# A fused two-block kernel on one core: the 3x3 convolution's taps as one chain on VectorE, without GpSimd's partial sums

## The chip, the cores and the metric

The kernel runs on one core of a Trainium2 chip, in one launch. The metric is the device time in microseconds (us). The engines are named as the profile names them: PE is TensorE's matmuls and PEld its weight loads, DVE is VectorE, ACT is ScalarE, POOL is GpSimd, SP is SyncE, which issues most DMAs. Each engine takes its instructions strictly in the order in which they stand in its queue.

## What is computed

Two transformer-like blocks over 512 tokens of width 1024. The first has two linear-attention branches, GLA (gated linear attention) and GDN (a gated delta rule), after a context of 256 tokens; the second is a sparse-attention layer, run twice, and is not touched here. The place of the change is the GDN branch's input:

```python
def conv_grid(u, w):                       # u: 512 tokens as an 8 x 64 grid, 1536 channels
    ug = u.reshape(b, rows, GRID_W, ch)
    out = lax.conv_general_dilated(ug, w[:, :, None, :], window_strides=(1, 1), padding='SAME', ...,
                                   feature_group_count=ch)
    return out.reshape(b, t, ch)

qkv = jnp.concatenate([bq, bk, bv], axis=-1)
qkv = jax.nn.silu(conv_grid(qkv, gdn_conv) if on_grid else conv_seq(qkv, gdn_conv))
bq = l2norm(qkv[..., :GDN_QK]...) * (GDN_DK ** -0.5)
bk = l2norm(qkv[..., GDN_QK:2 * GDN_QK]...)
bv = qkv[..., 2 * GDN_QK:]
```

Each channel is convolved with its own 3 x 3 taps, in float32. The context's tokens get a one-dimensional convolution of three taps (`conv_seq`). Behind it the delta rule needs, per chunk of 64 tokens, the products of k and q, the inverse of a triangular matrix, and a chain over the chunks.

## The kernel before, in words

Channels lie on the 128 partitions, so the 1536 convolved channels are 12 blocks, one per head and kind (4 of k, 4 of v, 4 of q). `conv_block` (L871) handles one: it loads and splits a weight tile (each float32 weight is split into a high and a low part, `split`, L188: ACT copies the high part, L190, and POOL or DVE subtracts, L193), projects the context and the 512 tokens on PE, and convolves. `convs` (L931) calls it for the heads of one half (`pp`), in the order k, v, q, and turns the results with PE transposes into the layouts that the delta rule wants. Two calls of `convs` alternate with two of `gla` in `first_block`: gla 0, convs 0, gla 1, convs 1; then `gla_out`, `gdn_scores`, `gdn_inverses`, `gdn_chains`, and the projections of gates (`fillers`, L485), which need only weights and the normed input.

The two-dimensional convolution of one block works on a zero-padded tile `xpad` of 10 x 66 per channel. ACT copies the projection into it (L897) and makes the centre tap from PSUM (L904). The other eight taps are on three engines: POOL makes the first tap (L908), the third (L914) and two additions (L915) into a partial sum `th`, ACT makes the second tap into `tap` (L912), DVE adds five taps one after the other (L918) and at the end the partial sum (L919). Then `silu2` (L395) runs a tanh on ACT (L398, into the same buffer `th`, which exists once) and a product on DVE (L399).

The GLA's levels (L837 to L861) put their differences and products on DVE (L837, L838, L840), exponentials on ACT and the keys' part on POOL (L847 to L850). `gdn_scores` (L984) loads rows of decays by DMA (L998, a buffer that exists once), subtracts and bounds them on DVE (L1030, L1032, L1037) and copies the scores KQ (L1020). `gla_out` scales the GLA's output on DVE (L623, transposed by PE right after) and multiplies it with its gate (L630). `gdn_inverses` is a chain of 62 small DVE operations that ends with two transposes (L1077).

The order of the instructions on each engine isn't that of the code: a scheduler places them when the program is built, with an estimate of its own of how long each takes (the `TileContext` of L1704). So a changed instruction moves others, on other engines too, as the section on the change shows.

Of the kernel before, what the change touches and what calls it, by code (L numbers as in the profile page):

```python
# [10 lines left out]
F32 = mybir.dt.float32  # L11
F32R = mybir.dt.float32r
I32 = mybir.dt.int32
AF = mybir.ActivationFunctionType
ALU = mybir.AluOpType
# [3 lines left out]
P = 128  # L19
D = 1024  # L20
KT = D // P
T = 512
# [210 lines left out]
def project(k, w, h, n=T, c0=0, tag="mm", step=None):  # L233

    ps = k.ps(tag)
    h = [x if isinstance(x, list) else [x[:, kt] for kt in range(x.shape[1])] for x in h]
    m = len(h[0])
    step = step or k.step
    for a in range(0, n, step):
        b = min(a + step, n)  # L240
        for kt in range(m):
            three(k, ps[:, a:b], w(kt, c0, P), [x[kt][:, a:b] for x in h], kt == 0, kt == m - 1)
    return ps[:, :n]
# [151 lines left out]
def silu2(k, out, x, tmp=None):  # L395

    tmp = out if tmp is None else tmp
    k.nc.scalar.activation(tmp, x, AF.Tanh, scale=0.5)  # L398
    k.nc.vector.scalar_tensor_tensor(out, tmp, 1.0, x, op0=ALU.add, op1=ALU.mult)  # L399
# [471 lines left out]
def conv_block(k, pool, win, hx, hc, blk, y, out, bank):  # L871


    nc = k.nc
    V, A, G = nc.vector, nc.scalar, nc.gpsimd
    w = Weights(k, win, [(1568 + P * blk, P, 0)])
    if hc is not None:
        th = k.t(pool, [P, T], F32, tag="th", bufs=1)
        pad = k.t(pool, [P, TC + 2], F32, tag="cpad", bufs=1)
        G.memset(pad[:, 0:1], 0.0)  # L880
        G.memset(pad[:, TC + 1:TC + 2], 0.0)
        A.copy(pad[:, 1:TC + 1], project(k, w, hc, TC, tag=bank))
        acc = y[:, :X0]
        for j in (1, 0, 2):
            s = k.conv[:, 3 + j, blk:blk + 1]
            if j == 1:
                V.tensor_scalar(acc, pad[:, j:j + TC], s, None, op0=ALU.mult)
            else:
                V.scalar_tensor_tensor(acc, pad[:, j:j + TC], s, acc, op0=ALU.mult, op1=ALU.add)
        silu2(k, acc, acc, th[:, :X0])  # L890
    pad = k.t(pool, [P, 10, 66], F32, tag="xpad", bufs=2)
    G.memset(pad[:, 0:1], 0.0)
    G.memset(pad[:, 9:10], 0.0)
    G.memset(pad[:, 1:9, 0:1], 0.0)
    G.memset(pad[:, 1:9, 65:66], 0.0)
    ps = project(k, w, hx, T, tag=bank).rearrange("p (r c) -> p r c", c=64)
    A.copy(pad[:, 1:9, 1:65], ps)  # L897

    def tap(j):
        return pad[:, j // 3:j // 3 + 8, j % 3:j % 3 + 64], k.conv[:, j, blk:blk + 1]  # L900

    acc = y[:, -T:].rearrange("p (r c) -> p r c", c=64)
    part = k.t(pool, [P, T], F32, tag="th", bufs=1).rearrange("p (r c) -> p r c", c=64)
    A.activation(acc, ps, AF.Copy, scale=tap(4)[1])  # L904
    for n, j in enumerate((0, 1, 2)):
        src, c = tap(j)
        if n == 0:
            G.tensor_scalar(part, src, c, 0.0, op0=ALU.mult, op1=ALU.add)  # L908
        else:
            one = k.t(pool, [P, T], F32, tag="tap", bufs=1).rearrange("p (r c) -> p r c", c=64)  # L910
            if n == 1:
                A.activation(one, src, AF.Copy, scale=c)  # L912
            else:
                G.tensor_scalar(one, src, c, 0.0, op0=ALU.mult, op1=ALU.add)  # L914
            G.tensor_tensor(part, part, one, op=ALU.add)  # L915
    for j in (3, 5, 6, 7, 8):
        src, c = tap(j)
        V.scalar_tensor_tensor(acc, src, c, acc, op0=ALU.mult, op1=ALU.add)  # L918
    V.tensor_tensor(acc, acc, part, op=ALU.add)  # L919
    a, b = y[:, -T:], k.t(pool, [P, T], F32, tag="th", bufs=1)  # L920
    if out is not None:
        a, b = (z.rearrange("p (t i) -> p t i", i=P) for z in (a, b))
    silu2(k, a if out is None else out, a, b)
# [7 lines left out]
def convs(k, pool, win, hx, hc, pp, s):  # L931
# [6 lines left out]
    for hd in (2 * pp, 2 * pp + 1):  # L938
        y = k.t(pool, [P, TA], F32, tag="y", bufs=2)
        conv_block(k, pool, win, hx, hc, 4 + hd, y, None, f"cm{pp}")  # L940
        rk = k.t(pool, [P, 6], F32, tag="rk", bufs=2)
        for a, n in ((0, 2), (2, 4)):
            ps = k.ps("tr")
            for t in range(n):
                tr(k, ps[:, t * P:(t + 1) * P], y[:, (a + t) * P:(a + t + 1) * P])
            for t in range(n):
                junk = k.t(pool, [P, NT, P], F32, tag="sq", bufs=1)[:, 0]
                A.activation(junk, ps[:, t * P:(t + 1) * P], AF.Square, accum_out=rk[:, a + t:a + t + 1])
            power(k, rk[:, a:a + n], rk[:, a:a + n], 1.0, 4 * EPS)
            V.tensor_tensor(kn[:, a:a + n, hd], ps[:, :n * P].rearrange("p (t d) -> p t d", d=P),  # L950
                            bc(rk[:, a:a + n, None], [P, n, P]), op=ALU.mult)
            ps = k.ps("tr")
            for t in range(n):
                tr(k, ps[:, t * P:(t + 1) * P], kn[:, a + t, hd])
            if a:
                A.copy(by_tile(kq[:, hd])[:, :, 0:4:3],
                       ps.rearrange("p (t u j) -> p t u j", u=2, j=64))
            else:
                A.copy(kc[:, hd], ps[:, :n * P])
    for hd in (2 * pp, 2 * pp + 1):  # L960
        y = k.t(pool, [P, TA], F32, tag="y", bufs=2)
        conv_block(k, pool, win, hx, hc, 8 + hd, y, None, f"cm{pp}")
        for a, n in ((0, 2), (2, 4)):
            ps = k.ps("tr")
            for t in range(n):
                tr(k, ps[:, t * P:(t + 1) * P], y[:, (a + t) * P:(a + t + 1) * P])
            A.activation(v[:, a:a + n, hd], ps[:, :n * P].rearrange("p (t d) -> p t d", d=P), AF.Copy, scale=0.5)
    for hd in (2 * pp, 2 * pp + 1):
        y = k.t(pool, [P, TA], F32, tag="y", bufs=2)
        q = by_tile(kq[:, hd])[:, :, 1:3].rearrange("p t u j -> p t (u j)")  # L970
        conv_block(k, pool, win, hx, None, hd, y[:, :T], q, f"cm{pp}")
        ps = k.ps("tr")
        sq = k.t(pool, [P, NT, P], F32, tag="sq", bufs=1)
        A.activation(sq, q, AF.Square)
        for t in range(NT):
            mm(k, ps[:, t:t + 1], sq[:, t], k.ones[:, 0:1])
        r = k.t(pool, [P, NT], F32, tag="rqh", bufs=2)
        power(k, r, ps[:, :NT], 1.0, 4 * EPS)
        for u in range(2):
            G.tensor_scalar(rq[64 - 64 * u:128 - 64 * u, :, hd], r[64 * u:64 * u + 64], 128.0 ** -0.5, 0.0,  # L980
                            op0=ALU.mult, op1=ALU.add)
# [726 lines left out]
```

## Time and profile before

| | |
|---|---|
| runs | 1330.84, 1329.47, 1330.38 us; median 1330.38 |
| profiled execution | 1328.28 us, span 1326.5 us, mean granted clock of TensorE 0.98 |
| PE busy | 1252.3 us, 94% |
| DVE busy | 867.2 us, 65% |
| ACT busy | 623.1 us, 47% |
| POOL busy | 431.8 us, 33% |

The span goes from the first to the last instruction of one profiled execution; that execution's own time is 1.8 us longer. A busy share is an average over stages with different limits; the stages are read with the view of windows. A group's row gives the mean of one instruction; the shortest one of a line shows what it takes undisturbed. Waits are put down to the instruction that came last.

### The profile page before, as it was taken

How to read it: one execution, taken by the hardware profiler on the slowest of the kernel's cores; microseconds unless marked ns; L12 is line 12 of the kernel's file. 1: busy time of each engine (PE TensorE's matmuls, PEld its weight loads, DVE VectorE, ACT ScalarE, POOL GpSimd, SP SyncE). 2: the span in 40 equal slices, each digit the busy share in tenths (PEclk: the TensorE clock that was granted, in tenths of full speed). 3: DMA queues.
4: the chain of work that ended last, by engine and by line, in shares of the span. 5: the costliest groups of instructions: out<-in, count | busy, mean ns of one | idle time of the engine just before them, and what ended most of it. 6: DMA issues, size and time to landing. Idle time of an engine off the chain costs nothing.

```text
span 1326.5 us, 22525 instructions
## 1 busy us (share of the span) xinstructions
PE 1252.3 (94%) x8290; PEld 1010.0 (76%) x8290; DVE 867.2 (65%) x1938; ACT 623.1 (47%) x1544; POOL 431.8 (33%) x469
## 2 busy tenths in 40 slices
PE   5998998989799999999899899999999999999997
PEld 1587987889799888587688778667777887667776
DVE  2748998698979974455767437654766537555664
ACT  2465445444452221244444336745655437645652
POOL 2416756376742322133423311111123311011131
PEclk9999999998999999999899999999999999999999
DMA  9421111202334321333553841012114631012121
GB/s 327 161 87 49 49 33 32 64 18 62 95 97 115 89 79 51 119 89 118 178 205 80 227 100 50 1 33 56 57 52 106 155 73 48 1 40 51 54 72 72
DMA packets 156766, 114.13 MB, mean 86 GB/s; under 512 B 37265, under 2 KB 137144, under 8 KB 156656
## 3 DMA queue, kind: packets, MB, share of 16 engines
q1 hardware_dynamic: 152888, 105.96, 27.8%
q10 hardware_dynamic: 3480, 6.65, 1.5%
q8 instruction: 65, 1.06, 0.3%
q14 instruction: 45, 0.37, 0.1%
q0 software_dynamic: 288, 0.09, 0.0%
HBM read 105.28 MB, written 10.27 MB: 87 GB/s over the span
## 4 chain that ended last, share of the span: by engine, by line
PE 71%; DVE 15%; DMA 4%; ACT 4%; issue 3%; POOL 2%; SPq 1%; POOLq 0%; ACTq 0%; DVEq 0%
PE A L172 30%; PE B L172 15%; PE C L172 9%; PE D L172 7%; PE E L172 6%; PE C L176 3%; DVE y L918 2%; DMA t<-w_mod 1%; DVE wlo L193 1%; DMA X<-cmp_w 1%; DVE aqe L823 1%; DVE att L861 1%; DVE a L838 1%; DVE a L837 1%; DVE a L840 1%
## 5 line engine op out<-in xcount | busy, mean ns | idle before, releaser
L172 PE MATMUL A<-t,whi 128*128 128x256 f32 (+1 forms) x1344 | 300.2, 314 | 3.7 <-DVE fill L399 2.2
L193 POOL TENSOR_TENSOR wlo<-wraw,whi 128x512 fp32r<-128x512 f32 x94 | 128.8, 1371 | 377.4 <-ACT whi L190 271.4
L190 ACT CAST whi<-wraw 128x512 fp32r<-128x512 f32 x226 | 139.1, 620 | 218.6 <-PE A L172 71.4
L172 PEld LDWEIGHTS A<-t,whi 128*128 128x128 f32 x1344 | 219.7, 191 | 24.4 <-issue 10.0
L172 PE MATMUL A<-t,wlo 128*128 128x256 f32 (+1 forms) x672 | 211.6, 315 | 0.7 <-POOL wlo L193 0.6
L193 DVE TENSOR_TENSOR wlo<-wraw,whi 128x512 fp32r<-128x512 f32 x132 | 107.3, 816 | 77.2 <-ACT whi L190 73.6
L172 PEld LDWEIGHTS A<-t,wlo 128*128 128x128 f32 x672 | 128.2, 191 | 14.2 <-issue 6.3
L172 PE MATMUL A<-whi,t 128*128 128x256 f32 (+1 forms) x544 | 122.0, 312 | 7.3 <-ACT av L765 4.4
L172 PE MATMUL C<-t,whi 128*128 128x256 f32 (+1 forms) x560 | 123.3, 311 | 0.0
L1436 ACT ACTIVATE X<-X,mx 128x256 f32<-128x256 f32 (+3 forms) x160 | 84.4, 528 | 41.2 <-DVE mx L1430 39.9
L172 PEld LDWEIGHTS A<-whi,t 128*128 128x128 f32 x544 | 90.9, 195 | 14.5 <-ACT av L765 4.8
L172 PEld LDWEIGHTS C<-t,whi 128*128 128x128 f32 x560 | 92.4, 193 | 6.6 <-issue 1.8
L172 PE MATMUL C<-t,wlo 128*128 128x256 f32 (+1 forms) x280 | 86.5, 310 | 0.0
L172 PE MATMUL A<-wlo,t 128*128 128x256 f32 (+1 forms) x272 | 83.7, 310 | 1.8 <-DVE wlo L193 1.6
L918 DVE SCALAR_TENSOR_TENSOR y<-xpad,t,y 128x512 f32<-128x512 f32 x60 | 65.2, 1087 | 4.6 <-ACT y L904 3.7
L176 PE MATMUL C<-t,X 128*128 128x128 f32 x352 | 57.8, 280 | 1.0 <-ACT pt L1447 0.4
L172 PEld LDWEIGHTS A<-wlo,t 128*128 128x128 f32 x272 | 53.1, 196 | 5.3 <-DVE wlo L193 2.2
L172 PEld LDWEIGHTS C<-t,wlo 128*128 128x128 f32 x280 | 54.1, 193 | 3.7 <-issue 1.4
L176 PEld LDWEIGHTS C<-t,X 128*128 128x128 f32 x352 | 40.2, 141 | 15.6 <-issue 6.5
L172 PE MATMUL B<-t,whi 128*128 128x512 f32 x144 | 47.6, 411 | 1.0 <-ACT whi L190 1.0
L1447 ACT COPY pt<-C 128x128 f32<-128x128 f32 (+3 forms) x96 | 39.0, 422 | 20.3 <-PE C L176 19.6
L1430 DVE CUSTOM_DVE_ANT_0 X<-B,t,sink 128x256 f32<-128x256 f32 (+1 forms) x64 | 27.1, 448 | 29.1 <-PE B L172 22.6
(621 smaller groups left out, 2811.4 us busy)
## 6 DMA issues: line engine op xcount, KB each, us to landing
wraw<-w_in SPq DMA_DIRECT2D x156, 256.0 KB
t<-w_mod SPq DMA_DIRECT2D x16, 512.0 KB
wraw<-w_out SPq DMA_DIRECT2D x32, 256.0 KB
t<-fill SPq DMA_DIRECT2D x20, 256.0 KB
wraw<-w_mod SPq DMA_DIRECT2D x16, 256.0 KB
wraw<-w_gdn_out SPq DMA_DIRECT2D x16, 256.0 KB
wraw<-w_o SPq DMA_DIRECT2D x16, 256.0 KB
X<-cmp_w SPq DMA_DIRECT2D x16, 256.0 KB
```

What stands on the lines that cost most here:

```text
L172: return k.nc.tensor.matmul(out, lhsT, rhs, start=start, stop=stop, **kw)
L176: return k.nc.tensor.transpose(out, in_, k.ident[:in_.shape[0], :in_.shape[0]])
L190: k.nc.scalar.copy(hi, raw)
L193: eng.tensor_tensor(lo, raw, hi.bitcast(F32), op=ALU.subtract)
L823: V.tensor_tensor(qe[64 * d:64 * d + 64, h], qT[hs], e[hs], op=ALU.mult)
L837: V.tensor_tensor(q4[:, :, 1], b4[:, :, 1], bmid, op=ALU.subtract)
L838: V.tensor_tensor(q4[:, :, 0], cmid, c4[:, :, 0], op=ALU.subtract)
L840: V.tensor_tensor(eq, eq, qT, op=ALU.mult)
L918: V.scalar_tensor_tensor(acc, src, c, acc, op0=ALU.mult, op1=ALU.add)
L1430: k.nc.vector.tensor_tensor_reduce(X[:, :n], ps[:, :n], mask, scale=-scale, scalar=first, op0=ALU.add, op1=ALU.min, accum_out=acc)
L1436: k.nc.scalar.activation(X, X, AF.Exp, bias=acc, scale=-1.0, accum_out=total)
L1447: k.nc.scalar.copy(pt[:, :n * P], ps[:, :n * P])
```

## The change

In `conv_block` all eight taps besides the centre become one chain of `scalar_tensor_tensor` on DVE. POOL's partial sum, ACT's second tap, their two buffers and DVE's last addition are gone. Per block that is three DVE operations more and one fewer, four POOL operations and one ACT operation fewer; there are 12 blocks. What is computed is the same sum in another order. Behind line 903 the changed kernel's line numbers are lower: L918 is L906 there, and from L919 on 13 less (L1030 is L1017, L1032 L1019, L1037 L1024, L1020 L1007).

```diff
     acc = y[:, -T:].rearrange("p (r c) -> p r c", c=64)
-    part = k.t(pool, [P, T], F32, tag="th", bufs=1).rearrange("p (r c) -> p r c", c=64)
     A.activation(acc, ps, AF.Copy, scale=tap(4)[1])
-    for n, j in enumerate((0, 1, 2)):
-        src, c = tap(j)
-        if n == 0:
-            G.tensor_scalar(part, src, c, 0.0, op0=ALU.mult, op1=ALU.add)
-        else:
-            one = k.t(pool, [P, T], F32, tag="tap", bufs=1).rearrange("p (r c) -> p r c", c=64)
-            if n == 1:
-                A.activation(one, src, AF.Copy, scale=c)
-            else:
-                G.tensor_scalar(one, src, c, 0.0, op0=ALU.mult, op1=ALU.add)
-            G.tensor_tensor(part, part, one, op=ALU.add)
-    for j in (3, 5, 6, 7, 8):
+    for j in (0, 1, 2, 3, 5, 6, 7, 8):
         src, c = tap(j)
         V.scalar_tensor_tensor(acc, src, c, acc, op0=ALU.mult, op1=ALU.add)
-    V.tensor_tensor(acc, acc, part, op=ALU.add)
```

The scheduler's order moves with it. First DVE, where the two q convolutions of the first half meet the start of the second GLA half (`ac` and `a` are the GLA's cumulated decays, L638 their first step). Before:

```order
L918 SCALAR_TENSOR_TENSOR y_1767<-xpad_1780,t_138,y_1767 128x512 x5
L919 TENSOR_TENSOR y_1767<-y_1767,th_1835 128x512
L399 SCALAR_TENSOR_TENSOR t_94<-th_1850,y_1767 128x4x128
L918 SCALAR_TENSOR_TENSOR y_1865<-xpad_1878,t_138,y_1865 128x512 x5
L256 TENSOR_SCALAR rqh_1860<-D_1853 128x4
L193 TENSOR_TENSOR wlo_2165<-wraw_2163,whi_2164 128x512
L638 SCALAR_TENSOR_TENSOR ac_351_1964<-a_355_1968 128x768
L919 TENSOR_TENSOR y_1865<-y_1865,th_1933 128x512
L399 SCALAR_TENSOR_TENSOR t_94<-th_1948,y_1865 128x4x128
L744 SCALAR_TENSOR_TENSOR a_355_1968<-a_355_1968,ac_351_1964 128x768
L638 SCALAR_TENSOR_TENSOR ac_350_1963<-a_354_1967 128x768
```

And now:

```order
L906 SCALAR_TENSOR_TENSOR y_1743<-xpad_1756,t_138,y_1743 128x512 x8
L906 SCALAR_TENSOR_TENSOR y_1835<-xpad_1848,t_138,y_1835 128x512 x2
L399 SCALAR_TENSOR_TENSOR t_94<-th_1820,y_1743 128x4x128
L906 SCALAR_TENSOR_TENSOR y_1835<-xpad_1848,t_138,y_1835 128x512 x2
L193 TENSOR_TENSOR wlo_2129<-wraw_2127,whi_2128 128x512
L906 SCALAR_TENSOR_TENSOR y_1835<-xpad_1848,t_138,y_1835 128x512 x2
L638 SCALAR_TENSOR_TENSOR ac_333_1928<-a_337_1932 128x768
L906 SCALAR_TENSOR_TENSOR y_1835<-xpad_1848,t_138,y_1835 128x512
L256 TENSOR_SCALAR rqh_1830<-D_1823 128x4
L906 SCALAR_TENSOR_TENSOR y_1835<-xpad_1848,t_138,y_1835 128x512
L638 SCALAR_TENSOR_TENSOR ac_332_1927<-a_336_1931 128x768
```

The GLA's first step stands behind 14 taps of the two convolutions where it stood behind 10 taps and an addition, its second behind all 16.

Second, DVE again, where the last q convolutions meet the delta rule's rows (`row`, by DMA) and the scaling of the GLA's output (`o`). Before, with all taps done:

```order
L1032 TENSOR_TENSOR L_3726<-row_3727,t_90 128x768
L1037 TENSOR_TENSOR AT_3770<-row_3727,t_90 128x512
L193 TENSOR_TENSOR wlo_3655<-wraw_3653,whi_3654 128x512
L399 SCALAR_TENSOR_TENSOR fill_3508<-fill_3508,A_3521 128x512
L1030 TENSOR_TENSOR row_3787<-row_3787,t_555 128x768
L623 TENSOR_TENSOR o_95<-o_95,t_3413 128x512 x4
```

And now:

```order
L1019 TENSOR_TENSOR L_3654<-row_3655,t_90 128x768
L1024 TENSOR_TENSOR AT_3698<-row_3655,t_90 128x512
L906 SCALAR_TENSOR_TENSOR y_3135<-xpad_3148,t_138,y_3135 128x512
L906 SCALAR_TENSOR_TENSOR y_3227<-xpad_3240,t_138,y_3227 128x512
L906 SCALAR_TENSOR_TENSOR y_3135<-xpad_3148,t_138,y_3135 128x512
L623 TENSOR_TENSOR o_95<-o_95,t_3341 128x512 x3
L906 SCALAR_TENSOR_TENSOR y_3227<-xpad_3240,t_138,y_3227 128x512
L623 TENSOR_TENSOR o_95<-o_95,t_3341 128x512
L193 TENSOR_TENSOR wlo_5150<-wraw_5148,whi_5149 128x512
L906 SCALAR_TENSOR_TENSOR y_3135<-xpad_3148,t_138,y_3135 128x512
L1017 TENSOR_TENSOR row_3715<-row_3715,t_555 128x768 x2
```

The scaling (L623) has gone ahead of the second tile of rows (`row_3787`, now `row_3715`), and taps of two convolutions stand between.

Third, PE, where it takes the first result of the inverses (`lt`) behind a gate's projection into bank A. Before:

```order
L172 MATMUL A_5978<-t_86,whi_5973 128x256
L172 MATMUL A_5978<-t_82,wlo_5974 128x256
L172 MATMUL A_5978<-t_82,whi_5973 128x256
L172 MATMUL A_5978<-t_86,whi_5973 128x256
L172 MATMUL B_3929<-lt_3921,L_3725 32x32 x24
```

And now (tile numbers are 72 lower here):

```order
L172 MATMUL A_5866<-t_3339,whi_5765 128x256
L172 MATMUL A_5866<-t_3335,wlo_5766 128x256
L172 MATMUL A_5866<-t_3335,whi_5771 128x256
L172 MATMUL A_5866<-t_3339,whi_5771 128x256
L172 MATMUL A_5866<-t_3335,wlo_5772 128x256
L172 MATMUL B_3857<-lt_3849,L_3653 32x32 x24
```

`A_5866` was `A_5938`, the tile ahead of `A_5978`. 9 of its 24 matmuls stand ahead of the inverses' result now; before it was all 24 and 23 of the next tile, 38 matmuls more.

## Rows read from the trace of the kernel before

**Rows 1.** The page's first part: busy time, share of the span, instructions.

```profile
PE 1252.3 (94%) x8290; PEld 1010.0 (76%) x8290; DVE 867.2 (65%) x1938; ACT 623.1 (47%) x1544; POOL 431.8 (33%) x469
```

**Rows 2.** Windows: length, then busy us (instructions) per engine; clock, DMA share, GB/s.

```profile
110.00:230.00 120.00, 107.00 (x807) 97.87 (x806) 110.06 (x157) 60.99 (x130) 80.82 (x96) 0.97 0.14 36
230.00:310.00 80.00, 75.59 (x560) 69.63 (x560) 67.73 (x106) 35.09 (x88) 43.94 (x55) 0.94 0.16 41
310.00:365.00 55.00, 46.63 (x371) 44.07 (x370) 46.59 (x53) 28.39 (x72) 41.80 (x37) 0.94 0.32 86
365.00:620.00 255.00, 254.50 (x2193) 213.11 (x2192) 169.71 (x370) 81.61 (x175) 75.71 (x78) 1.00 0.30 89
620.00:760.00 140.00, 127.38 (x712) 108.25 (x712) 93.79 (x163) 62.14 (x142) 46.46 (x49) 0.91 0.58 177
```

**Rows 3.** Waits of PE from 110 to 365 us: total us, times, longest.

```profile
PE E L172 <- DVE a L840: 4.3, 3, 2.4
PE B L176 <- DVE o L623: 3.3, 1, 3.3
PE D L176 <- DVE fill L630: 3.1, 1, 3.1
...
PE A L172 <- POOL wlo L193: 0.6, 1, 0.6
```

**Rows 4.** Groups by line and form, 100 to 345 us: busy us, mean ns | idle before.

```profile
L918 DVE SCALAR_TENSOR_TENSOR y<-xpad,t,y 128x512 f32<-128x512 f32 x60 | 65.2, 1087 | 4.6 <-ACT y L904 3.7
L837 DVE TENSOR_TENSOR a<-ac 128x256 f32<-128x256 f32 x14 | 12.2, 870 | 0.0
L919 DVE TENSOR_TENSOR y<-y,th 128x512 f32<-128x512 f32 x12 | 9.3, 778 | 1.8 <-POOL th L915 1.6
...
L915 POOL TENSOR_TENSOR th<-th,tap 128x512 f32<-128x512 f32 x24 | 36.1, 1504 | 1.6
L914 POOL TENSOR_SCALAR tap<-xpad,t 128x512 f32<-128x512 f32 x12 | 13.6, 1131 | 0.8
L908 POOL TENSOR_SCALAR th<-xpad,t 128x512 f32<-128x512 f32 x12 | 10.6, 885 | 29.7 <-DVE y L399 25.5 <-DVE t L399 4.2
...
L912 ACT ACTIVATE tap<-xpad,t 128x512 f32<-128x512 f32 x12 | 8.7, 722 | 8.0 <-POOL th L915 8.0
```

**Rows 5.** Single lines: duration ns min/median/max, first and last start us.

```profile
L918 DVE SCALAR_TENSOR_TENSOR y<-xpad,t,y x60: 728/954/1854, 119.9 to 333.9; 128x512 f32<-128x512 f32 x60
...
L837 DVE TENSOR_TENSOR a<-ac x14: 409/832/1537, 109.6 to 304.4; 128x256 f32<-128x256 f32 x14
```

**Rows 6.** Chain of waits (start us, us), then the timeline of POOL beside it.

```profile
191.27 1.66 DVE y L918
192.95 0.76 DVE y L918
...
190.78 1.58 POOL L915 TENSOR_TENSOR th<-th,tap 128x512 f32<-128x512 f32 x1
```

**Rows 7.** Waits of DVE from 110 to 395 us: total us, times, longest.

```profile
DVE KQ L1020 <- ACT KK L1019: 5.5, 5, 2.5
...
DVE y L918 <- ACT y L904: 3.7, 5, 1.1
DVE row L1030 <- DMA row<-t: 3.0, 1, 3.0
...
DVE y L919 <- POOL th L915: 1.6, 2, 1.2
```

**Rows 8.** Chain of waits: its stretch through POOL, first and last piece.

```profile
310.00 1.63 POOL wlo L193
...
324.31 1.79 DVE y L919
```

**Rows 9.** Timeline, 427 to 430 us: the inverses' first result and PE.

```profile
427.17 2.12 DVE L1077 STREAM_TRANSPOSE lt<-X 128x1024 f32<-128x1024 f32 x1
...
429.22 0.40 PE L172 MATMUL A<-t,whi 128*128 128x256 f32 x2
429.46 0.29 PE L172 MATMUL A<-t,wlo 128*128 128x256 f32 x1
...
429.91 0.28 PE L172 MATMUL B<-lt,L 32*32 32x32 f32 x5
```

## The prediction

> **What bounds the kernel now.** Read first the busy shares: TensorE (PE) works 94% of the span [rows 1], so little can be won that isn't PE standing still or PE's lower clock. Then read the stretches [rows 2]. The taps run from 119.9 to 333.9 us [rows 5], in the first three. There PE is busy 107.0 of 120, 75.6 of 80 and 46.6 of 55 us: 25.8 us idle. From 365 to 620 us PE is full, because the gate projections, which need nothing but weights, fill every hole. So the place to look is 110 to 365 us, and the neighbour to look at is VectorE (DVE), busy 110.1, 67.7 and 46.6 us there. In the first stretch it is busier than PE.
>
> Who holds PE up there? The waits [rows 3] name DVE: 4.3 us for the GLA level's product (L840), 3.3 us for the scaled GLA output (L623), 3.1 us for the output gate (L630). All of these stand in DVE's one queue, in which the convolution's taps stand too. And what holds DVE up? Its own list [rows 7] shows few large waits. The durations do it: a tap (L918) takes 1087 ns in the mean [rows 4] and 728 ns at its shortest [rows 5]. The chain of waits says when: two taps that follow each other take 0.76 and 1.66 us, and the long one starts at 191.27, with GpSimd (POOL) inside its 1.58 us addition of a partial sum (L915, from 190.78) [rows 6]. So POOL's help is paid for by DVE, in the same convolution.
>
> The second thing to see is that the chain also goes through POOL by itself: from 310.00 to 324.31 us it is POOL's weight split, its taps and its partial sums, until DVE's last addition [rows 8].
>
> Last, what follows. The inverses of the delta-rule blocks are a pure DVE chain. Their first result leaves DVE at 427.17 + 2.12 = 429.29 us, and PE takes it at 429.91 [rows 9]. PE has 0.6 us of room there, so a DVE that comes later to the inverses moves everything behind them. I therefore make the sum as DVE's time up to the inverses.
>
> **The change part by part.** All counts are for 12 convolutions, 110 to 395 us.
>
> *Added and removed on DVE.* 36 more taps at 0.728 us [rows 5] are 26.2 us. 12 final additions (L919) at 0.778 us [rows 4] go: 9.3 us. Net +16.9 us.
>
> *Relief.* POOL loses 24 additions (L915), 12 first taps (L908) and 12 last ones (L914): 36.1 + 10.6 + 13.6 = 60.3 us [rows 4]. What stood behind them in its queue, weight splits and the clearing of the next padded tile, comes earlier by that much; PE waits for POOL next to nowhere [rows 3], so I count nothing for it. What does DVE get back? The lower bound: the excess over the shortest is 60 x 0.359 = 21.5 us on L918 and 14 x (0.870 - 0.409) = 6.4 us on L837 [rows 4, 5], 27.9 us; POOL is busy 80.8 + 43.9 + 41.8 = 166.5 us there [rows 2], of which 60.3 is 36%; 36% of 27.9 is 10 us. The upper bound: all of L918's 21.5 and L919's wait of 1.6 [rows 7], 23 us. I take 20, near the upper end, because the partial sums run exactly beside their own convolution's taps [rows 6].
> On this the Trainium skill's page "SBUF — State Buffer", section "Who interferes with whom", says that a DVE instruction with two SBUF inputs and a GpSimd one that reads SBUF exclude each other, the second waiting until the first is done. Worked out from that alone, 48 POOL operations of 1.26 us, each blocking a tap for half its length, would give 30 us back and a sum of about -14 us. The rows allow no more than 23, so they decide.
>
> *The added taps are not free of POOL.* The weight splits (L193) and the GLA's keys stay on it. A third of the old excess, 0.12 us, on 36 taps is +4.3 us (bounds 0 and 36 x 0.359 = 12.9).
>
> *Waits of DVE.* L919's wait for POOL goes: 1.6 us. The order of L1030 and L623 turns round: the second pair of L1030, whose rows come by DMA and cost 3.0 us of waiting, now stands behind the four L623 and five taps, so the 3.0 us are covered, and PE's 3.3 us for L623 with them. Taps now also stand between the copies KQ (L1020), which waited 5.5 us for ScalarE (ACT); I take half, 2.7. The first tap waits for ACT's centre tap, 3.7 us in all [rows 7]; ACT loses 12 taps of 722 ns (8.7 us) [rows 4], which stood in its queue and waited for POOL; half of it, 1.8. Together -9.1 us (bounds 0 and -13.8). ACT's 8.7 us count for nothing else: it is half idle, and if it were not, 8.7 us would be the most that comes back.
>
> Where this falls: before the second GLA half, 18 of the extra taps stand ahead of its first products (48 taps instead of 30); ahead of its last level it is 72 instead of 48. The other 12 come between that and the inverses, in the holes of the delta rule's scores.
>
> DVE reaches the inverses at 16.9 - 20 + 4.3 - 9.1 = -7.9 us.
>
> *PE behind it.* PE's own order changes too: 38 matmuls of a gate projection that stood ahead of the first inverse's result now stand behind it; at 0.12 us, the distance at which such matmuls start [rows 9], 4.6 us. If PE is full until 620 us, they cost all of that; if they fall into the 12.6 us that PE stands idle in 620 to 760 [rows 2], nothing. I take 4, since PE is full that long.
>
> *DMA.* None is added or taken. On the SP queue two more weight loads come ahead of the second row load; no wait for a weight load stands among the waits of PE or of DVE [rows 3, 7], so they cost nothing unless the rows come later than the five taps and four L623 ahead of them, which is the 3.0 us again. POOL issues no DMA here.
>
> Sum: -7.9 + 4 = -3.9, say **-4 us**. The profiled execution took 1328.28 us (span 1326.5 and 1.8 around it); the median of the runs is 1330.38, 2.1 more. So 1324.3 on the profile's scale, **1326.4 us** as a median.
>
> **The rivals.**
> *A. DVE becomes the bound (slower).* The relief is only the lower bound's 10 us, because POOL's splits and key products move up into the room, and of the waits only the DMA's 3.0 us goes: 16.9 - 10 + 4.3 - 3.0 = +8.2 us. It would be seen at PE's first take of the inverse, which has 0.6 us of room [rows 9]; the shifted matmuls then fall into PE's wait and cost nothing more. 1338.6 us. It decides once relief and vanished waits together are below 21.2 us. For it: DVE is busy 110 of 120 us in the first stretch [rows 2]. Against: taps of 1.66 us stand where POOL adds [rows 6].
> The Trainium skill's page "Perfetto Trace Analysis", section "Optimizing Scalar/DVE Operations", speaks for this rival with its advice to move work to ScalarE or even GpSimd when DVE is saturated, and against it in the same paragraph, since the two share a read port and moving between them might not help.
>
> *B. It comes out even.* DVE gains what the shifted matmuls cost, 4.6 us, and PE is full behind it: 0, 1330.4 us. For it: PE at 254.5 of 255 us from 365 to 620 [rows 2].
>
> *C. A larger gain.* All the waits of [rows 7] go and the relief is 23: 16.9 - 23 + 4.3 - 13.8 = -15.6, half the shifted matmuls (+2.3): -13 us, 1317.4 us. PE's idle 25.8 us has room for it. For it: the chain through POOL of 14 us at 310 [rows 8] holds one convolution, whose eight taps on DVE alone would take 8 x 0.73 = 5.8. Against: PE was at work beside most of it.
>
> That the change doesn't do what it says is excluded: the new order has 96 taps on DVE and none on POOL.
>
> **How the numbers follow.** A measurement of this kernel can tell about 0.2%, 2.7 us, from no change. The forecast (its own range -9 to 0) gets 0.42, A 0.26, B 0.17, C 0.15. Faster by over 0.2%: three quarters of the forecast and C, 0.46. Slower: A and small parts of the others, 0.31. Within: 0.23. The range 1315 to 1339 leaves out A with added taps at their full excess (0.10), the lower part of C (0.06) and some 0.03 for stray effects of the new order. The forecast's own range is 1321 to 1330.
>
> **What would show it.** Right: the mean of the taps falls from 1087 to about 850 ns; L837 and the other GLA rows get shorter; L1030's DMA wait and PE's wait for L623 are gone; the inverse's L1077 ends some 8 us earlier than 429.29 us. Wrong: L1077 ends later than 429 us with PE waiting right behind it (A); taps still above 0.95 us in the mean (A); L1077 earlier but PE idle no less after 620 us, or more (B, or a loss that I don't see). If the taps get short and the time still doesn't fall, the step that fails is that DVE's time is the kernel's.

## The result and the profile after

The change makes the kernel slower. In the first measurement the changed kernel took 1338.66 us (median) against 1330.61 for the kernel before (one run more than in the table above), a ratio of 1.0053 with a 95% interval of [1.0038, 1.0068]; measured again beside the experiments (run e14) it took 1336.98 against 1331.92, 1.0035 [1.0021, 1.0048]. The loss is 5 to 8 us. The changed kernel's first profiled execution's span is 1336.2 us, 9.7 more than before. L918 is L906 now, L904 is L903, and lines from 919 on are 13 lower.

The page's first part answers to [rows 1]:

```profile
PE 1252.2 (94%) x8290; PEld 1011.7 (76%) x8290; DVE 866.8 (65%) x1962; ACT 614.5 (46%) x1532; POOL 368.0 (28%) x421
```

PE is busy as long as before, to 0.1 us, in these two executions. So all of the 9.7 us is PE standing still. The view of windows says where; it answers to [rows 2] (length, then busy us and instructions of PE, PEld, DVE, ACT, POOL; clock, DMA share, GB/s):

```profile
110.00:230.00 120.00, 110.93 (x828) 101.50 (x828) 112.66 (x172) 58.70 (x126) 49.79 (x72) 0.96 0.14 36
230.00:310.00 80.00, 77.86 (x588) 72.05 (x587) 64.10 (x108) 32.37 (x84) 27.05 (x42) 0.96 0.18 47
310.00:365.00 55.00, 40.50 (x322) 37.85 (x320) 46.02 (x58) 26.89 (x70) 21.09 (x17) 0.82 0.29 77
365.00:620.00 255.00, 249.18 (x2135) 210.32 (x2136) 171.14 (x367) 77.35 (x164) 79.15 (x87) 0.97 0.29 86
620.00:760.00 140.00, 124.17 (x736) 107.02 (x735) 89.18 (x157) 60.67 (x145) 45.45 (x46) 0.91 0.54 170
```

From 110 to 310 us PE is idle 11.2 us where it was 17.4: the change has won 6.2 us there. From 310 to 365 it is idle 14.5 where it was 8.4, from 365 to 620 it is 5.8 where it was 0.5, and from 620 to 760 it is 15.8 where it was 12.6: 14.6 us lost, 6.2 won. Behind 760 us another 1.4 us are lost. The 3.2 us from 620 to 760 are in the main one wait of PE, for DVE's L548 at the end of the delta rule's chains, which has grown from 5.6 to 8.7 us; no run here tells why. Most of the loss lies in 30 us. The same window of both kernels, before first:

```profile
345.00:375.00 30.00, 23.07 (x197) 21.18 (x196) 24.00 (x30) 11.98 (x23) 20.97 (x17) 0.89 0.32 84
```

```profile
345.00:375.00 30.00, 13.72 (x81) 11.16 (x80) 26.20 (x37) 10.13 (x18) 13.32 (x14) 0.50 0.10 26
```

PE does 81 matmuls instead of 197 there. It was busy 2.6 of the 5 us from 340 to 345, and from 345 us on the granted clock is 0.50, the lower of its two levels (1.2 GHz), for the whole stretch.

The taps did what was expected of them. The groups from 100 to 345 us, which answer to [rows 4]:

```profile
L906 DVE SCALAR_TENSOR_TENSOR y<-xpad,t,y 128x512 f32<-128x512 f32 x87 | 71.0, 819 | 3.4 <-ACT y L903 2.5
...
L837 DVE TENSOR_TENSOR a<-ac 128x256 f32<-128x256 f32 x14 | 8.3, 592 | 1.1 <-PE B L172 1.1
```

A tap takes 819 ns in the mean where it took 1087 (87 of the 96 taps lie in this window; over all of them it is 834), an L837 592 where it took 870. What is new is in the waits of PE from 110 to 365 us, which answer to [rows 3] (total us, times, longest):

```profile
PE E L172 <- DVE KQ L1007: 9.2, 1, 9.2
PE A L172 <- ACT av L765: 3.8, 3, 3.2
PE B L176 <- DVE o L623: 2.4, 2, 1.6
```

The old waits have shrunk, and one new wait of 9.2 us is larger than their gain. The timeline of PE, then of DVE, shows it (start us, us, engine, line; in brackets the idle time ahead and what ended it):

```profile
359.50 1.98 PE L172 MATMUL E<-t 128*64 128x128 f32 x16 [9.17 <-DVE KQ L1007]
361.46 1.87 PE L172 MATMUL D<-t,sq 128*128 128x1 f32 x8
367.37 0.98 PE L172 MATMUL D<-t,sq 128*128 128x1 f32 x4 [4.04 <-DVE rqh L256]
```

```profile
352.88 0.94 DVE L1019 TENSOR_TENSOR L<-row,t 128x768 f32<-128x768 f32 x1
353.75 0.68 DVE L1024 TENSOR_TENSOR AT<-row,t 128x512 f32<-128x512 f32 x1
354.35 1.98 DVE L906 SCALAR_TENSOR_TENSOR y<-xpad,t,y 128x512 f32<-128x512 f32 x1
356.26 0.41 DVE L1007 COPY KQ<-E 64x256 f32<-64x256 f32 x1
356.59 2.30 DVE L906 SCALAR_TENSOR_TENSOR y<-xpad,t,y 128x512 f32<-128x512 f32 x2
358.93 0.43 DVE L1007 COPY KQ<-E 64x256 f32<-64x256 f32 x1
```

The product of k and q lies in bank E, which has one buffer; DVE empties it with two copies KQ that stand in its queue between taps of the last q convolutions, and DVE hasn't a gap. Behind that, PE needs the norms of these q (D<-t,sq), which need the same taps; the second norm waits 4.04 us until DVE has read the first out of bank D (L256), and that stands in DVE's queue behind the last tap, two copies KQ and two products L1023.

Why do taps stand there at all? Before, the last one started at 333.9 us; now at 361.4. The view of windows with DVE alone, before first:

```profile
295.00:335.00 40.00, 34.72 (x43) 0.87 0.23 60
335.00:365.00 30.00, 26.87 (x34) 0.89 0.36 95
```

```profile
295.00:335.00 40.00, 28.44 (x41) 0.91 0.28 74
335.00:365.00 30.00, 29.50 (x38) 0.66 0.26 70
```

DVE stood idle 11.6 us of the 40 ahead of the stretch in which it is full, where it was 5.3 before. It idles there in pieces, of which the largest are 3.9 us for ACT's half of the weight splits (L190) and 2.1 for PE's scores. The work was not too much, it came too late. The timeline leads to the cause. DVE's part of the scaling of the second half's first k head (its reciprocal norm in L256, then the product L937, L950 before), before first:

```profile
268.24 0.17 DVE L256 TENSOR_SCALAR rk<-rk 128x4 f32<-128x4 f32 x1 [0.53 <-ACT sq L948]
...
270.14 0.69 DVE L950 TENSOR_TENSOR t<-D,rk 128x512 f32<-128x512 f32 x1
```

```profile
275.25 0.58 DVE L256 TENSOR_SCALAR rk<-rk 128x4 f32<-128x4 f32 x1
277.43 0.75 DVE L906 SCALAR_TENSOR_TENSOR y<-xpad,t,y 128x512 f32<-128x512 f32 x1
279.33 1.15 DVE L906 SCALAR_TENSOR_TENSOR y<-xpad,t,y 128x512 f32<-128x512 f32 x1
280.40 0.68 DVE L937 TENSOR_TENSOR t<-D,rk 128x512 f32<-128x512 f32 x1
```

Before, DVE waited 0.53 us for the squares and took them at once. Now the squares are done at 271.4, and the scaling comes 10 us later than it did. Four taps of the next convolution stand between, 3.7 us, and nine other operations of the GLA, the context and the splits, which the new order has put there too. The product empties bank D, which has one buffer too and takes every transpose of k and v and the column sums of the q norms in turn. The second k head's first scaling comes 12 us later than it did, its last transposes 15 us later, at 304.90 instead of 289.81, and only with these its `y`, of which there are two, comes free for the tenth convolution. The rows of DVE, PE and ACT, before:

```profile
284.65 0.41 DVE L950 TENSOR_TENSOR t<-D,rk 128x256 f32<-128x256 f32 x1
289.81 0.60 PE L176 MATMUL D<-t,y 128*128 128x128 f32 x4
297.95 0.70 ACT L904 ACTIVATE y<-C,t 128x512 f32<-128x512 f32 x1
```

And in the changed kernel, with DVE's first instruction of the tenth convolution (L887), which waited for these transposes:

```profile
296.83 0.41 DVE L937 TENSOR_TENSOR t<-D,rk 128x256 f32<-128x256 f32 x1
304.90 0.49 PE L176 MATMUL D<-t,y 128*128 128x128 f32 x3
305.86 0.68 ACT L903 ACTIVATE y<-C,t 128x512 f32<-128x512 f32 x1
305.54 0.36 DVE L887 TENSOR_SCALAR y<-cpad,t 128x256 f32<-128x256 f32 x1 [0.37 <-PE D L176]
```

The tenth convolution's centre tap (L903) starts at 305.86, 8 us later than before (297.95), though the ninth's was 7.6 us earlier (275.8 against 283.4). The eleventh and the twelfth follow 9 and 5 us late.

### The profile page after: what moved, and what is told of

The parts are those of the page before. It is cut to its first block, busy times and chain, and to the rows that moved or that the text cites. A ratio compares the mean times of both kernels' runs of the same rounds, so it can differ in the third digit from the quotient of the medians.

```text
span 1336.2 us, 22475 instructions
## 1 busy us (share of the span) xinstructions
PE 1252.2 (94%) x8290; PEld 1011.7 (76%) x8290; DVE 866.8 (65%) x1962; ACT 614.5 (46%) x1532; POOL 368.0 (28%) x421
## 4 chain that ended last, share of the span: by engine, by line
PE 76%; DVE 13%; ACT 3%; DMA 3%; issue 3%; POOL 1%; ACTq 0%; SPq 0%; POOLq 0%; DVEq 0%
PE A L172 30%; PE B L172 17%; PE C L172 9%; PE D L172 8%; PE E L172 7%; PE C L176 4%; DVE y L906 2%; DMA t<-w_mod 1%; DMA wraw<-w_gdn_out 1%; DVE a L838 1%; DVE a L840 1%; DVE aqe L823 1%; DVE wlo L193 1%; DVE att L861 1%; DVE ac L747 1%
## 5 line engine op out<-in xcount | busy, mean ns | idle before, releaser
L190 ACT CAST whi<-wraw 128x512 fp32r<-128x512 f32 x226 | 138.7, 619 | 227.3 <-PE A L172 71.6
L193 DVE TENSOR_TENSOR wlo<-wraw,whi 128x512 fp32r<-128x512 f32 x132 | 110.3, 840 | 89.2 <-ACT whi L190 85.6
L906 DVE SCALAR_TENSOR_TENSOR y<-xpad,t,y 128x512 f32<-128x512 f32 x96 | 79.7, 834 | 3.5 <-ACT y L903 2.5
L176 PEld LDWEIGHTS C<-t,X 128*128 128x128 f32 x352 | 40.2, 141 | 15.6 <-issue 6.5
```

Of the source, the lines that this page charges most:

```text
L176: return k.nc.tensor.transpose(out, in_, k.ident[:in_.shape[0], :in_.shape[0]])
L190: k.nc.scalar.copy(hi, raw)
L193: eng.tensor_tensor(lo, raw, hi.bitcast(F32), op=ALU.subtract)
```

## The experiments

Each ratio is to runs of the kernel before that were taken beside it on the same chip. The last three columns are read from the profiled execution of each: the start of the tenth centre tap, the start of the last tap, and DVE's busy time from 295 to 335 us. In e6 and e7, with another order of the convolutions, the tenth is a q head.

| run | us | ratio [95% interval] | tenth | last | DVE |
|---|---|---|---|---|---|
| before | 1331.20 to 1331.92 | 1 | 298.0 | 333.9 | 34.7 |
| the change (e14) | 1336.98 | 1.0035 [1.0021, 1.0048] | 304.3 | 360.3 | 28.3 |
| e1 first half only | 1329.05 | 0.9983 [0.9968, 0.9997] | 293.5 | 328.0 | 36.9 |
| e2 second half only | 1341.65 | 1.0075 [1.0057, 1.0093] | 311.4 | 367.0 | 28.3 |
| e3 KQ on ACT | 1335.48 | 1.0027 [1.0015, 1.0039] | 306.7 | 366.2 | 28.3 |
| e4 last q shared | 1340.86 | 1.0071 [1.0053, 1.0089] | 307.0 | 359.5 | 28.6 |
| e5 KQ on ACT, norms late | 1338.16 | 1.0052 [1.0034, 1.0069] | 304.4 | 364.2 | 28.6 |
| e6 order k, q, v | 1332.34 | 0.9997 [0.9983, 1.0012] | 298.5 | 340.0 | 34.4 |
| e7 before, order k, q, v | 1332.01 | 1.0002 [0.9989, 1.0015] | 300.7 | 337.5 | 34.4 |
| e8 norms late | 1340.62 | 1.0065 [1.0050, 1.0080] | 304.9 | 361.6 | 28.6 |
| e9 three y | 1328.25 | 0.9974 [0.9963, 0.9986] | 293.1 | 333.7 | 36.9 |
| e10 control of e9 | 1333.71 | 1.0029 [1.0012, 1.0046] | 305.2 | 361.1 | 28.2 |
| e11 k's scaling on ACT | 1318.77 | 0.9904 [0.9882, 0.9927] | 292.2 | 340.2 | 36.3 |
| e12 before, k's scaling on ACT | 1328.29 | 0.9971 [0.9957, 0.9986] | 298.2 | 343.0 | 31.0 |
| e13 e9 and e11 together | 1332.99 | 0.9995 [0.9980, 1.0010] | 294.2 | 332.1 | 35.7 |

The table falls into two groups, though within the second the times still differ, e11's and e13's by 14 us. Where the tenth centre tap comes after 304 us, DVE is busy 28.2 to 28.6 us in its idle stretch and the kernel is slower than before; where it comes by 301, DVE is busy 31.0 us or more, and no kernel is measurably slower.

### Which convolutions lose the time

Where `shared` holds, a block keeps the partial sums of the kernel before; the condition is e1's, and in e2 it is `blk % 4 < 2`, in e4 `blk in (2, 3)`:

```diff
+    shared = blk % 4 >= 2
+    if shared:
+        part = k.t(pool, [P, T], F32, tag="th", bufs=1).rearrange("p (r c) -> p r c", c=64)
...
+    else:
+        for j in (0, 1, 2, 3, 5, 6, 7, 8):
```

> The change in the first half's six convolutions only; the second half's six keep the partial sums. Order theory (the loss of 8 us comes only from the last two q convolutions' taps standing among the copies KQ): here no tap stands between those copies, so the wait of PE for KQ on bank E is gone and only the gain of the first half is left: 1326 to 1328.5 us, PE idle no more than before from 110 to 310 us. Rival (VectorE has too much work everywhere, each convolution costs its share of the 8.3 us): half of the loss, about 1334.5 us.

> The change in the second half's six convolutions only; the first half's six keep the partial sums. Order theory: taps of the last q convolutions stand among the KQ copies as in the change, so PE waits there 8 to 10 us for KQ, and without the first half's gain the whole is 1338 to 1342 us, at least as slow as the full change. Rival (a share per convolution): about 1334.5 us, as the other half.

The two halves aren't alike, so a price per convolution is out: the first half alone gains 0.17% (interval 0.03 to 0.32%), which is half a us above its range, and no wait for KQ is left in its trace; the second alone loses 0.75%, as expected, and PE waits 10.0 us there for KQ. e1 also holds both kinds of tap in one kernel (groups from 100 to 345 us; L926 are the taps alone, L921 those with partial sums beside them):

```profile
L926 DVE SCALAR_TENSOR_TENSOR y<-xpad,t,y 128x512 f32<-128x512 f32 x48 | 38.6, 806 | 0.7
...
L921 DVE SCALAR_TENSOR_TENSOR y<-xpad,t,y 128x512 f32<-128x512 f32 x30 | 32.5, 1084 | 2.3 <-ACT y L906 1.9
```

0.28 us per tap is what a convolution with POOL's partial sums costs DVE. It isn't the half of the kernel that does it: e2 has the two kinds the other way round and shows 1116 ns with the sums and 839 without.

> The full change except the last two q convolutions, which keep the partial sums: the ten others on VectorE alone. The order still has the last taps and additions between the KQ copies, but 10 taps and 2 additions instead of 16 taps after the projection of the last q. Order theory: PE still waits for KQ, by some 4 us less than 9.2, so 1332 to 1336 us. Rival 1 (a share per convolution): 8.3 x 10/12 = 6.9, 1337 us. Rival 2 (the number of taps of the last two convolutions alone decides, not where they stand): the loss is gone, 1325 to 1328 us.

A miss for all three: with 10 taps and 2 additions instead of 16 taps in the last two convolutions the kernel is no faster than the change. The number of taps there doesn't decide. The wait for KQ did shrink, to 4.1 us, but PE waits 10.5 us for the squares of these q heads instead. The tenth convolution is as late as in the change.

### Is it the wait that the profile names?

The first pair of lines is in e3 and e5; in e5 and e8 the squares, column sums and powers of the second half's q heads move from `convs` into a function `q_norms` that is called behind `gdn_scores`:

```diff
-            V.tensor_copy(KQ[part(u), :, 2 * tp:2 * tp + 2], pv[part(u), :, :, 64 - 64 * u:128 - 64 * u])
+            A.copy(KQ[part(u), :, 2 * tp:2 * tp + 2], pv[part(u), :, :, 64 - 64 * u:128 - 64 * u])
...
             AT = [gdn_scores(k, gp, gates, pp, s, Ls) for pp in range(2)]
+            q_norms(k, gp, fp, s)
```

> The full change, with the four copies KQ of each half moved from VectorE to ScalarE, right behind the copies KK; taps are as in the change. Order theory: bank E is given free without VectorE's queue, the wait of 9.2 us for KQ goes, the 24 taps and small operations behind it run beside PE's fillers: 1327 to 1332 us. Rival (VectorE's work up to the inverses is the bound): the same work stands ahead of the first inverse's result, PE waits there in place of KQ, 1336 to 1339 us.

> The full change, with the norms of the last two q heads issued behind the scores, KQ left on VectorE. Order theory: the norm's wait of 4 us at 363 us goes, the wait for KQ of 9 us stays, so 1333 to 1337 us. Rival (VectorE's length): 1336 to 1339 us.

> As the run with KQ on ScalarE, and the norms of the last two q heads (square, column sum on PE, power) are issued behind the scores instead of inside the convolutions. All 96 taps stay on VectorE where the change has them. Order theory, sharpened (PE loses the time because instructions that need the last taps stand in its queue ahead of gate projections that need nothing): neither KQ nor a norm is left there, PE's idle time from 345 to 375 us falls from 16 to below 8 us, and the whole is 1326 to 1330 us. Rival (VectorE's length up to the inverses is the bound): PE waits at the inverses' first result instead, 1335 to 1339 us.

The order theory missed in all three: they took 1335.5, 1340.6 and 1338.2 us where it had at most 1332, 1337 and 1330. The rival, VectorE's length up to the inverses, has the time in e5 and misses it by less than 2 us in e3 and e8, yet the wait that it named, PE's at the inverses' first result, stands in none of the three traces. The longest wait of PE from 345 to 375 us, in e3, then in e5:

```profile
PE D L172 <- ACT sq L961: 13.1, 2, 11.2
```

```profile
PE A L172 <- DVE fill L399: 16.7, 1, 16.7
```

The wait for KQ goes, and PE waits at the norms instead; the norms go, and it waits at the gate projections, which I had taken for free of all this. They aren't: bank A is emptied by a tanh on ACT and a product on DVE. In e5, ACT's tanh of the gate stands behind the tanh of the last convolution:

```profile
365.05 0.63 ACT L398 ACTIVATE th<-y 128x512 f32<-128x512 f32 x1 [7.04 <-DVE y L907]
367.16 0.60 ACT L398 ACTIVATE fill<-A 128x512 f32<-128x512 f32 x1 [1.48 <-DVE t L193]
```

So KQ is only the place at which PE meets the late taps first. The theory that named KQ and the norms falls; what is left is that the last taps are late, whichever of these PE meets first.

### Is it too much work on DVE, or its place?

In `convs` the three loops over k, v and q stand in the order k, q, v, in e6 in the changed kernel and in e7 in the kernel before:

```diff
-        conv_block(k, pool, win, hx, hc, 8 + hd, y, None, f"cm{pp}")
+        conv_block(k, pool, win, hx, None, hd, y[:, :T], q, f"cm{pp}")
...
-        conv_block(k, pool, win, hx, None, hd, y[:, :T], q, f"cm{pp}")
+        conv_block(k, pool, win, hx, hc, 8 + hd, y, None, f"cm{pp}")
```

> The full change, with the convolutions of each half called in the order k, q, v. Not one instruction more or fewer; all 96 taps are on VectorE, but now ahead of the copies KQ, and the q norms ahead of the scores. Order theory: the waits for KQ and for the norms are gone, 1326 to 1330 us. Rival (VectorE's work is the bound): as the change, 1336 to 1340 us.

> Control: the kernel before, with its partial sums, in the order k, q, v. There is no tangle to mend here, so the order theory expects no more than small changes, 1328 to 1334 us. If this order by itself gained 8 us or more, the gain of the changed kernel in that order would say nothing of the taps.

With not one instruction more or fewer the loss is gone (0.9997), and the order by itself gives the kernel before nothing (1.0002). So the loss isn't DVE's amount of work. It took 1332.3 where at most 1330 was expected: PE's idle time from 310 to 375 us is 9.6 us, near the 8.9 of the kernel before, but the change's gain ahead of it is gone too (17.6 us idle from 110 to 310, where the change has 11.2), in part to a new wait of 5.2 us at 228 us.

### Why the last convolutions are late

e9 gives `y` a third buffer and moves the squares to make room; e10 has the moved squares alone:

```diff
-        y = k.t(pool, [P, TA], F32, tag="y", bufs=2)
+        y = k.t(pool, [P, TA], F32, tag="y", bufs=3)
...
-                junk = k.t(pool, [P, NT, P], F32, tag="sq", bufs=1)[:, 0]
+                junk = k.t(pool, [P, P], F32, tag="junk", bufs=1)
...
-        sq = k.t(pool, [P, NT, P], F32, tag="sq", bufs=1)
+        sq = k.t(pool, [P, T], F32, tag="th", bufs=1).rearrange("p (t i) -> p t i", i=P)
```

e11 (the change) and e12 (the kernel before) leave `y` alone and scale the k heads on ACT; e13 is the change with the edits of e9 and e11:

```diff
-            V.tensor_tensor(kn[:, a:a + n, hd], ps[:, :n * P].rearrange("p (t d) -> p t d", d=P),
-                            bc(rk[:, a:a + n, None], [P, n, P]), op=ALU.mult)
+            for t in range(n):
+                A.activation(kn[:, a + t, hd], ps[:, t * P:(t + 1) * P], AF.Copy, scale=rk[:, a + t:a + t + 1])
```

> The full change with a third buffer for the convolutions' result y. Room for it: the squares of a q head go into th, those of a k head into a small tile of their own; the tile tap is gone with the change. New theory (the last two q convolutions come late because their y waits for a buffer that the second k head's turns through bank D still hold; so VectorE, idle before, has its taps from 334 to 361 us, where everything on PE needs VectorE): the last tap ends before 345 us, PE is idle less than 9 us from 345 to 375 us, the whole 1322 to 1331 us. Rival (VectorE's work up to the inverses is the bound wherever the taps stand): 1335 to 1340 us.

> Control for the third buffer: the same moves of the squares, but two buffers for y as in the change. The taps stand among the copies KQ as in the change. New theory and rival both expect the change's time, 1336 to 1341 us; were it below 1333, the squares' place and not the buffer would be the cause.

> The full change, y with two buffers, but the scaling of the k heads from PSUM (which on VectorE stood behind taps, 10 us later than before at 280 us) is done by ScalarE, one 128x128 piece per instruction. New theory (that scaling, late in VectorE's queue, holds bank D, this holds y, and this the last convolutions): bank D turns faster, the last tap ends before 350 us, 1326 to 1333 us. Rival (VectorE's work is the bound): 8 operations, 4.5 us by their lengths in the changed kernel, less on VectorE, so no better than 1334 us.

The third buffer alone (e9 beside e10) brings the tenth centre tap from 305.2 to 293.1, the last tap from 361.1 to 333.7, and the kernel from 0.29% above to 0.26% below the kernel before. DVE in e9, in the windows that stand above for the others:

```profile
295.00:335.00 40.00, 36.94 (x54) 1.00 0.29 72
335.00:365.00 30.00, 28.17 (x36) 0.74 0.29 72
```

Its busy time has gone back to where it was idle. In e9 bank D is as late as in the change (the two scalings come at 282.2 and 303.2 us), the second k head's last transposes even later, and the tenth centre tap doesn't wait for them any more:

```profile
293.13 0.69 ACT L903 ACTIVATE y<-C,t 128x512 f32<-128x512 f32 x1
309.19 0.66 PE L176 MATMUL D<-t,y 128*128 128x128 f32 x4
```

So it is the buffer `y` through which the late bank costs time. Both edits act in both halves, but at the seventh centre tap e9 is 4 us behind e10 (249.3 against 245.0), so what it gains it gains after that. Not all of its time is accounted for: PE's idle time from 310 to 375 us falls from 21.8 (e10) to 12.7 us, but 3.9 us of it come back ahead of 310 us and 4.3 behind 620, and over the whole PE is idle 82.3 us against 82.9. Of the 3.8 us between the two spans 3.2 are PE's busy time, which differs from run to run with the same 8290 matmuls (1245.5 us in e9, 1248.7 in e10, 1257.7 in e6); why, no run here tells. Two numbers missed: e9's PE was idle 11.6 us from 345 to 375, not under 9, and e10 stood at 1333.7, a little below the range. The other remedy, at the cause that the rows show, does more, and more than was expected: with k's scaling out of DVE's queue the second k head's last transposes start at 288.4, the tenth centre tap at 292.2, and the kernel takes 1318.8 us, 0.96% less than before.

> Control: the kernel before, with its partial sums, and the k heads' scaling from PSUM on ScalarE. If the taps' place in VectorE's queue is what the scaling mends in the changed kernel, there is less to mend here: 1326 to 1332 us, so that the taps on VectorE alone are worth 7 us or more beside it. Rival (the moved scaling gains by itself, whatever the taps do): 1317 to 1322 us, and the taps are worth nothing.

Part of e11 may be the moved scaling itself, which gives 0.29% on the kernel before, where it does nothing to the tenth centre tap (298.2 against 298.0). In this pair of runs the rest, 0.9904 / 0.9971 = 0.993 or some 9 us, goes with the taps on DVE; e13, which has the same taps and the same scaling, doesn't have it, so it is not a price of the taps by themselves. e11's trace can't show where it comes from: it is of the slowest of its six executions (1324.2 us), and PE is idle in it as long as before (73.7 against 74.2 us).

> The change with both remedies, three buffers for y and the k heads' scaling on ScalarE. If both mend the same wait, the second adds nothing: 1316 to 1324 us. If they mend two, their gains over the change, 10 and 20 us, add: 1309 to 1313 us.

> The change itself once more, timed beside the two controls on the same chip: 1336 to 1340 us by the first measurement.

e14 repeats the change's time as expected. Neither outcome of e13 came. Its tenth convolution is early and its last tap too, but the time is that of the kernel before. It waits elsewhere, above all here, where e11 waits 4.0 us and the change 8.7:

```profile
PE D L176 <- DVE o L548: 13.2, 1, 13.2
```

That is the end of the delta rule's chains, from 654 us on, far from the convolutions. Why the gain is lost there I haven't tested; it stays open. e1, e9 and e11 are faster than the kernel before, and e11 is the fastest.

## Why the prediction was wrong

I forecast 1326.4 us and a faster kernel; it is 5 to 8 us slower, at 1338.66 just inside the range.

**The durations were right.** 36 added taps at the measured 0.834 us (79.7 us for 96 in the whole kernel) are 30.0 us; I had 26.2 + 4.3. The relief, by the means, is 60 x (1087 - 834) = 15.2 us on the taps and 14 x (870 - 592) = 3.9 on L837, 19.1 us; I had 20. With the 9.3 us of the removed additions that is +1.6 us; I had +1.2. DVE's busy time from 110 us to the inverses' transpose even fell, from 277.0 to 274.0 us; rows that I hadn't counted went both ways (the 16 context taps L889 from 818 to 515 ns, the 14 L840 from 869 to 998). The rule of the Trainium skill's page "SBUF — State Buffer", section "Who interferes with whom", that the second of the two engines waits until the first is done, points the right way: e1 shows 0.28 us per tap between the two kinds. The 30 us estimated from it are more than the 19.1 that the rows gave.

**The step that failed** is the waits: "Together -9.1 us", and the sentence under where it falls, "The other 12 come between that and the inverses, in the holes of the delta rule's scores." DVE's idle time up to the inverses, which should have shrunk by 9.1 us, grew from 40.2 to 48.9, by 8.7. The four waits that I counted fell from 13.8 to 9.3 us, by 4.5 (L919's is gone, L1030's went from 3.0 to 1.6, the centre tap's from 3.7 to 2.5, KQ's only from 5.5 to 5.2). Another grew by 9.5, DVE's for ACT's half of the weight splits, before first:

```profile
DVE wlo L193 <- ACT whi L190: 6.0, 4, 3.4
```

```profile
DVE wlo L193 <- ACT whi L190: 15.5, 8, 5.7
```

By place, 6.3 us of idle time were added from 295 to 335 us, ahead of the late taps, and 7.1 from 365 us on, behind them; 4.7 went elsewhere. I priced only waits that the trace of before showed. I didn't ask who stands *behind* an added tap: the k heads' scaling, which holds bank D, which holds `y`, which holds the tenth convolution. The prediction's sum treated DVE's list as something that only gets longer or shorter. The inverses' transpose L1064 starts at 432.86 us, 5.7 later than L1077's 427.17, where I had 8 us earlier.

**The place of the bound was wrong.** I looked for DVE's lateness at PE's first take of the inverse, with 0.6 us of room. In the change PE goes from a gate's matmul straight to it:

```profile
435.37 0.28 PE L172 MATMUL A<-t,wlo 128*128 128x256 f32 x1
435.58 0.81 PE L172 MATMUL B<-lt,L 32*32 32x32 f32 x39
```

It doesn't wait there, though L1064 ends later than 429 us; it had waited 9.2 and 4.0 us at 350 and 363. And the gate projections, which I had as needing nothing but weights, need bank A emptied by ACT and DVE too: in e5 PE waits 16.7 us for that.

**Rival A** gave 1338.6 us, but not by what happened, and that the number fits is chance: its relief of only 10 us didn't come true, and e6 and e9 show that the same 96 taps fit. **Rival C** named the room that PE's idle time up to 365 us leaves; e11 comes near its 1317.4 us with one more edit, but its trace has only 7.4 us less idle time than before from 110 to 375 us and as much more behind, so it isn't shown that C's room is what it used. **The 4 us for the shifted matmuls** can't be told apart in these runs.

**The signs that I named** were mixed, as their last sentence allowed: the taps got short, L1030's DMA wait fell to 1.6 us and the wait for L623 to 2.4, and the time didn't fall. "The step that fails is that DVE's time is the kernel's" is then only half of it: DVE's amount of work wasn't the kernel's time, its order was.

## What to carry to other kernels

When work is added to an engine's queue, ask of each neighbour that it is put ahead of what that neighbour sets free: here it was worth more than the change cost to move one small operation that empties a single PSUM bank. Look for idle time of the engine just ahead of the stretch in which it is full; if it is there, try an earlier start (a buffer, another order, that one operation on another engine) ahead of less work; here each of the three took the loss away. And don't trust the instruction that the waits name until it has been taken away: here PE found the next one behind the same taps, twice.

## What the runs showed that I had not expected

- A wait that goes can leave the time where it is: without KQ's 9.2 us PE waited 11.2 us at the norms, without these 16.7 us for bank A.
- Calling the convolutions in another order (e6 against the change) is worth about 0.4% with the same instructions, on a kernel whose PE is 94% busy.
- Two remedies that each gain (0.26% below the kernel before, and 0.96%) gave nothing measurable together (0.9995, interval 0.9980 to 1.0010).
- With PE idle for more than half of the 30 us from 345 us on, the granted clock was 0.50 there, and still PE's busy time in the whole kernel was unchanged (1252.3 and 1252.2 us).
